# Edges loaded quad by quad ahead of the node features, and the first pass's keys, codes and feature casts put in another order

## The chip, the cores and the metric

The kernel runs on one core of one Trainium2 chip. A core has TensorE (matmuls; PE in the profile, PEld for its weight loads), VectorE (DVE), ScalarE (ACT), GpSimd (POOL) and SyncE (SP, which only issues DMAs here), each with its own instruction queue, which it works off in order. The metric is the device time of one execution in microseconds (us), the median of several runs.

## The reference

The inputs are 4096 node rows of 128 float32 numbers and 65,536 edges, each with a random source and a random destination node.

```python
output = np.zeros((num_nodes, dim), dtype=np.float32)
for i in range(len(edge_index_src)):
    output[edge_index_dst[i]] += node_features[edge_index_src[i]]
```

## The kernel before

The kernel sorts the edges by destination block and source block (32 blocks of 128 nodes each), with matmuls against one-hot matrices, and then multiplies the node features by 0/1 count matrices. Everything that the change touches lies in `_fast`, whose order on every engine is the order of the code (a manual schedule).

Loads. 128 partitions hold 512 edges each, as 64-bit numbers of which the low word counts. One DMA on SP's queue brings the destinations (`rawd`, L100), one on ScalarE's queue the sources (`raws`, L101). Right behind the destinations SP issues four DMAs of 512 KB for the node features X (`xf`, L109). VectorE fills the pads behind the edges (L102, L103).

Constants. `keep_busy(WARM)` runs 60 matmuls on a tile of ones whose result nobody reads (L127). GpSimd makes triangular matrices and iotas (L130 to L142), VectorE copies the iotas into a PSUM tile `psi` (L144 to L147), and GpSimd zeroes those parts of the two permutation tiles `p1` that no one-hot writes (L152 to L158): eight memsets.

Pass 1 sorts the edges in six "quads" q of up to 88 columns (22 groups of 4). For each quad: `dst_keys(q)` (VectorE) shifts the destinations to block numbers `kd`; `buckets1(q)` (VectorE, L210 with output `oh`) compares them with the iota, 128x2816 one-hot; `column_sums1(q)` (TensorE, 22 matmuls, L227) sums it, `scan(q)` (VectorE, L236) makes running sums; `counts(q)` is a generator that `count(q, n)` moves on by n steps: six steps of matmuls (L245, L249) with one ScalarE activation each (L252, `cum`), then 32 matmuls (L257, `psr`) and two ScalarE copies (L261) that give `rank1[q]`. `spread1(q)` (GpSimd, L273, four products) multiplies the one-hot by the words `kab` that `codes()` makes from both edge lists (VectorE L178 to L182, ScalarE L185). `move1(q)` makes the permutation one-hots in `p1` (VectorE, twelve L210 rows with output `p`) and permutes with TensorE (L296); ScalarE takes the result to `sbk` and `sa` (L300, L301). `move1` calls `during(q)`, which lays the next quads' counts and, with `beside`, pass 2's first group in between.

`x_part(i, 0)` casts a quarter of X on ScalarE (L195, 1 instruction); `x_part(i, 1)` makes its residual on GpSimd (L199, 2 instructions). They are needed when the products begin (L696), in the order of i.

The order ahead of the loop over `move1` is written out at L340 to L363. The code behind it is pass 2 (groups of destination blocks) and, from L767 on, 32 slots of one-hot (VectorE), block matmul (L689), ScalarE cast to `a` (L691) and product (L696).

Of the kernel before, what the change touches and what calls it, by code (L numbers as in the profile page):

```python
# [8 lines left out]
P = 128  # L9
F32 = mybir.dt.float32  # L10
F32R = mybir.dt.float32r
BF16 = mybir.dt.bfloat16
I32 = mybir.dt.int32
# [4 lines left out]
NB = 32  # L18
NCH = 24
NJ = 22  # L20
NH = NCH // 2
NQ = NCH // 4
# [1 line left out]
CODE0 = 0x2000  # L24
BIG = 4096.0
GROUPS = (4,) * 8
WARM = 60

LATER = (1, 3)
WHOLE = (1, 2)  # L30
# [6 lines left out]
WIN = ((0, 7, 0, 64), (7, 14, 4, 100), (14, NJ, 20, P))  # L37
# [45 lines left out]
def _fast(ctx, tc, X, src32, dst32, out, ident, fmax, flag_i, T):  # L83
# [13 lines left out]
    raws = raw[:, 2 * NT:4 * NT].rearrange("p (t w) -> p t w", w=2)  # L97
    code_i = raw[:, 4 * NT:].bitcast(U16)[:, :NT]
    sblk_i = raw[:, 4 * NT:].bitcast(U16)[:, NT:]
    nc.sync.dma_start(out=rawd[:, :T, :], in_=bass.AP(dst32, 0, [[2 * T, P], [2, T], [1, 2]]))  # L100
    nc.scalar.dma_start(out=raws[:, :T, :], in_=bass.AP(src32, 0, [[2 * T, P], [2, T], [1, 2]]))  # L101
    V.memset(rawd[:, T:, :], 4096)  # L102
    V.memset(raws[:, T:, :], 0)  # L103
    NX = 4
    BX = NB // NX
    xft = sb1.tile([P, NX, BX, P], F32, name="xf", tag="F")
    xf = [xft[:, i] for i in range(NX)]
    for i in range(NX):
        nc.sync.dma_start(out=xf[i], in_=X[i * BX * P:(i + 1) * BX * P, :].rearrange(  # L109
            "(s p) f -> p s f", p=P))  # L110


    identb = sb1.tile([P, P], BF16, name="identb")
# [4 lines left out]
    one = sb1.tile([P, 1], F32, name="one")  # L118
    iota = sb1.tile([P, P], U16, name="iota")
    iotas = sb1.tile([P, P], U16, name="iotas")  # L120
    V.tensor_copy(out=identb[:], in_=ident[:])
    G.memset(ones[:], 1.0)

    def keep_busy(n):
        psw = ps.tile([P, 512], F32, name="psw", tag="psA", bufs=4)
        for i in range(n):
            PE.matmul(out=psw[:, :P], lhsT=ones[:], rhs=ones[:], start=True, stop=True)  # L127

    keep_busy(WARM)
    G.affine_select(out=before[:], in_=ones[:], pattern=[[1, P]], base=0,  # L130
                    channel_multiplier=-1, compare_op=OP.is_gt, fill=0.0)
    G.affine_select(out=early[:], in_=before[:], pattern=[[1, P]], base=0,
# [9 lines left out]
    G.iota(iotax[:], pattern=[[2, NB // 2], [-1, 2]], base=1, channel_multiplier=0)  # L142
    psi = ps.tile([P, 4, P // 2], I32, name="psi", tag="psi", bufs=1)
    V.tensor_copy(out=psi[:, 0], in_=iota[:].bitcast(I32))  # L144
    V.tensor_copy(out=psi[:, 1], in_=iotas[:].bitcast(I32))
    V.tensor_copy(out=psi[:, 2], in_=iota4[:].rearrange("p s k -> p (s k)").bitcast(I32))
    V.tensor_copy(out=psi[:, 3, :NB // 2],  # L147
                  in_=iotax[:].rearrange("p s k -> p (s k)").bitcast(I32))
    piota, piotas = psi[:, 0].bitcast(U16), psi[:, 1].bitcast(U16)
    pswap = psi[:, 3].bitcast(U16)  # L150

    p1 = [sb1.tile([P, 2, NJ, P], BF16, name=f"p1{i}", tag=f"t2{i}") for i in range(2)]  # L152
    for t in p1:
        for j0, j1, m0, m1 in WIN:
            if m0 > 0:
                G.memset(t[:, :, j0:j1, :m0], 0.0)
            if m1 < P:
                G.memset(t[:, :, j0:j1, m1:], 0.0)  # L158

    p2a = sb1.tile([P, 2, NCH, P], BF16, name="p2a")  # L160

# [4 lines left out]
    kab = sb1.tile([P, NQ, NL], F32, name="kab", tag="K1")  # L166

    def by_quad(t):
        return t.rearrange("p (j q l) -> p q j l", q=NQ, l=4)

    def dst_keys(q):
        V.tensor_single_scalar(
            out=kd[:, q].rearrange("p (j l) k -> p j l k", l=4),
            in_=by_quad(d_lo)[:, q, :, :, None].to_broadcast([P, NJ, 4, 2]),
            scalar=7, op=OP.logical_shift_right)

    def codes():
        V.tensor_scalar(out=code_i, in0=s_lo, scalar1=127, scalar2=7,  # L178
                        op0=OP.bitwise_and, op1=OP.logical_shift_left)
        V.scalar_tensor_tensor(out=code_i, in0=d_lo, scalar=127, in1=code_i,  # L180
                               op0=OP.bitwise_and, op1=OP.bitwise_or)
        V.tensor_single_scalar(out=sblk_i, in_=s_lo, scalar=7, op=OP.logical_shift_right)  # L182
        words = kab[:].rearrange("p q n -> p (q n)")
        for dt, k, v, bias in ((U16, 1, code_i, CODE0), (BF16, 0, sblk_i, 1)):
            S.activation(  # L185
                out=words.bitcast(dt).rearrange("p (q j l k) -> p q j l k", q=NQ, l=4, k=2)[..., k],
                in_=by_quad(v), func=COPY, bias=float(bias))


    xr = [sb1.tile([P, NB // 2, 2, P], F32R, name=f"xr{h}") for h in range(2)]  # L190

    def x_part(i, v):
        blks = slice(i % 2 * BX, (i % 2 + 1) * BX)
        if v == 0:
            S.copy(out=xr[i // 2][:, blks, 0, :], in_=xf[i])  # L195
        else:
            for h in range(2):
                bs = slice(i % 2 * BX + h * BX // 2, i % 2 * BX + (h + 1) * BX // 2)
                G.tensor_tensor(out=xr[i // 2][:, bs, 1, :], op=OP.subtract,  # L199
                                in0=xf[i][:, h * BX // 2:(h + 1) * BX // 2],  # L200
                                in1=xr[i // 2][:, bs, 0, :])
# [16 lines left out]
    def buckets1(q):  # L218

        if q % 2 == 0:  # L220
            oh1[q // 2] = sb1.tile([P, 2, NL, NB], BF16, name="oh1", tag=f"o{q // 2}")
        onehot(oh1q(q), kd[:, q], NL, NB, io=pswap if q % 2 else piota)

    def column_sums1(q):
        pst = ps.tile([P, 512], F32, name="pst", tag=("ps2", "pso")[q % 2], bufs=1)
        for j in range(NJ):
            PE.matmul(out=pst[:, j:j + 1],  # L227
                      lhsT=oh1q(q)[:, 4 * j:4 * j + 4, :].rearrange("p l b -> p (l b)"),
                      rhs=ones[:, :1], start=True, stop=True)
        sums[q] = pst  # L230

    def scan(q):

        pst = sums[q]
        sums[q] = sb2.tile([P, NJ], BF16, name="sums")
        V.tensor_tensor_scan(out=sums[q][:], data0=ones[:, :NJ], data1=pst[:, :NJ], initial=0.0,  # L236
                             op0=OP.mult, op1=OP.add)
# [25 lines left out]
    def count(q, n=99):  # L263
        for _ in range(n):
            next(counting[q], None)
# [3 lines left out]
    def spread1(q):  # L269

        v1[q] = sb1.tile([P, NL, NB], F32, name="v1", tag=f"A{q % 2}")
        for l in range(4):
            G.tensor_tensor(out=v1[q][:, l::4], in0=oh1q(q)[:, l::4], op=OP.mult,  # L273
                            in1=kab[:, q, l::4, None].to_broadcast([P, NJ, NB]))
# [10 lines left out]
    def move1(q, meanwhile):  # L285
        tag, bufs = ("psA", 4) if q == NQ - 2 else ("misc", 1)
        psm = ps.tile([P, 512], F32, name="psm", tag=tag, bufs=bufs)
        for l in range(4):
            t = p1[l // 2]
            n = len([j for j in range(NJ) if j * NCH + q * 4 + l < T])  # L290
            for j0, j1, m0, m1 in WIN:
                j1 = min(j1, n)
                onehot(t[:, l % 2, j0:j1, m0:m1], rank1[q][:, l, j0:j1], j1 - j0, m1 - m0, m0=m0)
            meanwhile(l)
            for j in range(n):
                PE.matmul(out=psm[:, l * 64:(l + 1) * 64], lhsT=t[:, l % 2, j, :],  # L296
                          rhs=v1[q][:, 4 * j + l].bitcast(BF16),
                          start=j == 0, stop=j == n - 1)
        pv = psm[:, :256].rearrange("p (l b k) -> p l b k", l=4, k=2)
        S.copy(out=sbk[:, place(q), :], in_=pv[:, :, :, 0])  # L300
        S.copy(out=sa[:, place(q), :], in_=pv[:, :, :, 1])  # L301
# [37 lines left out]

    dst_keys(0)  # L340
    buckets1(0)
    column_sums1(0)
    x_part(0, 0)
    codes()
    scan(0)
    for q in range(1, NQ):
        dst_keys(q)
    spread1(0)
    count(0, 6)
    buckets1(1)  # L350
    column_sums1(1)
    spread1(1)
    buckets1(2)
# [1 line left out]
    scan(1)  # L355
    column_sums1(2)
    buckets1(3)
    x_part(0, 1)
    count(1, 6)
    x_part(1, 0)  # L360
    scan(2)
    column_sums1(3)
    x_part(1, 1)  # L363

    keys2 = {}
    p2b = [p2a[:, 0], p2a[:, 1]]
# [95 lines left out]
    def beside(q, l):  # L462

        if q == 2 and l == 2:
            start0()
            buckets0(0)
            buckets0(1)
        if q == 2 and l == 3:
            scan0(0)
            scan0(1)  # L470
        if q == 3 and l == 0:
            counts0(0)
            counts0(1)
        if q in (3, 4):
            if l == 1:
                buckets0(q - 1)
            if l == 2:
                scan0(q - 1)
            if l == 3:
                counts0(q - 1)  # L480
        if q == 5:
            if l == 1:
                ranks0(EARLY0[0], T0["x"][:, 384:], 2)
            if l == 2:
                buckets0(4)

    def during(q):

# [13 lines left out]
    for q in range(NQ):  # L502
        if q == NQ - 1:
            p2c = sb1.tile([P, 2, NCH, P], BF16, name="p2c", tag="o2")
            p2b += [p2c[:, 0], p2c[:, 1]]
        move1(q, during(q))
        if q + 4 < NQ:
            buckets1(q + 4)
            column_sums1(q + 4)
        if q < 2:  # L510
            x_part(q + 2, 0)
        if q + 2 < NQ:
            spread1(q + 2)

# [220 lines left out]
    for cs in EARLY0:  # L735
        permute0(0, cs)
    buckets0(NQ - 1)
    scan0(NQ - 1)
    counts0(NQ - 1)
    ranks0(place(4), T0["x"][:, 384:])  # L740
# [167 lines left out]
```

## Time and profile before

| | us |
|---|---|
| median of 3 runs | 277.62 (277.42 to 277.76) |
| the profiled execution | 277.6 |
| its span on the core | 275.9 |
| PE / DVE / ACT / POOL busy | 264.7 / 241.3 / 188.7 / 197.2 |
| all DMA | 3.15 MB read, 2.10 MB written |

The span runs from the first to the last recorded instruction; 1.7 us of the execution lie around it. Busy time of PE counts pipelined matmuls by modelled ends, so a busy PE is not a PE at its peak. A share over the whole span mixes the opening, pass 1, and the slots, which have different limits; the views below are therefore taken by stage. A row of the time line merges neighbouring instructions of one form: start, time, engine, line, operation, output and inputs, count, and in brackets the idle time before it and what ended that.

### The profile page before, as it was taken

Reading aid. Unit: us, or ns where it says so; the run is one execution under the profiler, and the core shown is the slowest. Engines: PE = TensorE matmul, PEld = TensorE weight load, DVE = VectorE, ACT = ScalarE, POOL = GpSimd, SP = SyncE. Lnnn points to the kernel's source line nnn. Section 1 sums busy time; section 2 is a strip of 40 time slices with the busy share of each in tenths; the row PEclk is TensorE's granted clock in tenths of the full one; section 3 lists DMA queues with packets and bytes.
Section 4 is the critical chain, followed back from the end, with each engine's and each line's share of the span. In section 5 each row is a group of like instructions: output and inputs, shape, how many; then the busy total and the mean of one; then the engine's idle time right before and its main releaser. Section 6 shows DMA issues by size and latency. Waiting matters only on the chain.

```text
span 275.9 us, 8028 instructions
## 1 busy us (share of the span) xinstructions
PE 264.7 (96%) x3466; PEld 223.3 (81%) x3466; DVE 241.3 (87%) x241; ACT 188.7 (68%) x403; POOL 197.2 (71%) x205
## 2 busy tenths in 40 slices
PE   7599999998999999999999999999999999999994
PEld 7488888986888888888888888888888788888872
DVE  3989986999999989999999999899898899889601
ACT  1867777247576857777668686857776776777761
POOL 7499999849599999999899998999699400000000
PEclk9999999999999999999999999999999999999998
DMA  7900000000000010001000100100010001001001
GB/s 229 230 2 4 5 4 4 2 5 0 2 2 1 2 40 0 2 1 40 2 0 2 38 2 1 40 4 0 2 38 2 0 2 38 2 0 40 0 5 39
DMA packets 8725, 5.77 MB, mean 21 GB/s; under 512 B 240, under 2 KB 8432, under 8 KB 8688
## 3 DMA queue, kind: packets, MB, share of 16 engines
q1 hardware_dynamic: 8272, 4.59, 5.9%
q10 hardware_dynamic: 416, 0.66, 0.8%
q8 instruction: 27, 0.44, 0.7%
q14 instruction: 10, 0.08, 0.1%
HBM read 3.15 MB, written 2.10 MB: 19 GB/s over the span
## 4 chain that ended last, share of the span: by engine, by line
PE 86%; ACT 5%; DVE 5%; DMA 2%; issue 1%; DVEq 0%; ACTq 0%
PE pso L696 44%; PE psa L689 20%; PE ps L616 4%; PE psm L296 3%; ACT cum L252 3%; PE psr L257 2%; PE psr L600 2%; DVE p L210 2%; DMA raw<-in_edge_index_dst_dram 2%; PE psb L565 2%; PE psc L249 2%; PE psc L245 2%; ACT cum L649 1%; PE psx L315 1%; DVE oh L210 1%
## 5 line engine op out<-in xcount | busy, mean ns | idle before, releaser
L691 ACT CAST a<-psa 128x512 fp32r<-128x512 f32 x256 | 131.7, 604 | 25.8 <-PE psa L689 25.7
L696 PE MATMUL pso<-a,xr 128*128 128x512 f32 x512 | 133.6, 403 | 0.2
L696 PEld LDWEIGHTS pso<-a,xr 128*128 128x128 f32 x512 | 91.0, 188 | 17.6 <-ACT a L691 1.6
L210 DVE TENSOR_TENSOR oh<-psi,slo 128x4096 bf16<-128x4096 uint16 (+1 forms) x34 | 73.4, 2159 | 8.2 <-PE psa L689 8.2
L210 DVE TENSOR_TENSOR oh<-psi,dlo 128x4096 bf16<-128x4096 uint16 (+1 forms) x34 | 73.3, 2155 | 0.0
L689 PE MATMUL psa<-oh 128*128 128x128 bf16 x1024 | 68.5, 219 | 0.6 <-ACT cum L649 0.6
L689 PEld LDWEIGHTS <-oh 128*128 128x128 bf16 x1024 | 58.0, 98 | 12.5 <-issue 12.2
L548 POOL TENSOR_TENSOR v<-oh,sa 128x512 bf16<-128x512 bf16 x42 | 42.7, 1054 | 1.8 <-DVE oh L539 1.8
L587 POOL TENSOR_TENSOR cum<-cum,oh 128x512 bf16<-128x512 bf16 x36 | 40.6, 1169 | 0.0
L273 POOL TENSOR_TENSOR v<-oh,kab 128x704 f32<-128x704 bf16 x24 | 32.9, 1403 | 5.5 <-ACT kab L185 4.4
L210 DVE TENSOR_TENSOR p<-psi,rank 128x448 bf16<-128x448 uint16 (+3 forms) x72 | 29.6, 479 | 0.0
L252 ACT ACTIVATE cum<-psc,minus 128x512 bf16<-128x512 f32 (+1 forms) x36 | 21.0, 650 | 2.4 <-PE psc L249 1.7
L578 POOL TENSOR_TENSOR cum<-cum,two 128x256 bf16<-128x256 bf16 x25 | 19.3, 770 | 4.5 <-ACT cum L567 2.9
L296 PE MATMUL psm<-v,p 128*128 128x64 bf16 x512 | 18.2, 193 | 0.2
L555 POOL TENSOR_TENSOR two<-oh 128x512 bf16<-128x512 bf16 x15 | 17.0, 1168 | 1.1 <-DVE oh L539 1.1
L296 PEld LDWEIGHTS <-p 128*128 128x128 bf16 x512 | 16.7, 98 | 0.4 <-issue 0.4
L582 POOL TENSOR_TENSOR cum<-cum,oh 128x512 bf16<-128x512 bf16 x15 | 17.0, 1164 | 0.0
L210 DVE TENSOR_TENSOR p2a<-psi,rank 128x3072 bf16<-128x3072 uint16 (+2 forms) x14 | 14.4, 1063 | 0.9 <-ACT rank L604 0.8
L210 DVE TENSOR_TENSOR p2c<-psi,rank 128x3072 bf16<-128x3072 uint16 x8 | 13.6, 1746 | 0.0
L249 PEld LDWEIGHTS <-sums 128*128 128x128 bf16 x126 | 10.0, 98 | 4.5 <-DVE sums L236 0.9
L249 PE MATMUL psc<-identb,sums 128*128 128x128 bf16 x126 | 12.6, 219 | 0.6 <-DVE sums L236 0.6
L245 PE MATMUL psc<-oh,early 128*128 128x512 bf16 (+1 forms) x36 | 13.0, 361 | 0.0
(105 smaller groups left out, 241.3 us busy)
## 6 DMA issues: line engine op xcount, KB each, us to landing
xf<-in_node_features_dram SPq DMA_DIRECT2D x4, 512.0 KB, 7.5
out_dram<-rows SPq DMA_DIRECT2D x7, 256.0 KB, 2.3
raw<-in_edge_index_src_dram ACTq DMA_DIRECT2D x1, 512.0 KB, 4.8
raw<-in_edge_index_dst_dram SPq DMA_DIRECT2D x1, 512.0 KB, 5.1
out_dram<-rows SPq DMA_DIRECT2D x1, 128.0 KB, 1.8
out_dram<-rows ACTq DMA_DIRECT2D x1, 128.0 KB, 2.1
```

What stands on the lines that cost most here:

```text
L210: V.tensor_tensor(out=dst.rearrange("p i (m k) -> p i m k", k=2), in0=io.rearrange("p i (m k) -> p i m k", k=2), in1=keys2[:, :, None, :]. ...
L245: PE.matmul(out=psc[:, :n * P], lhsT=early[:], rhs=oh1q(q)[:, 4 * j0:4 * (j0 + n), :].rearrange("p t b -> p (t b)"), start=True, stop=j0 + ...
L249: PE.matmul(out=psc[:, (j - j0) * P:(j - j0 + 1) * P], lhsT=sums[q][:, j - 1:j].to_broadcast([P, P]), rhs=identb[:], start=False, stop=j = ...
L252: S.activation(out=cum[:, :, 4 * j0:4 * (j0 + n)], func=RELU, bias=minus[:], in_=psc[:, :n * P].rearrange("p (t b) -> p b t", b=NB))
L273: G.tensor_tensor(out=v1[q][:, l::4], in0=oh1q(q)[:, l::4], op=OP.mult, in1=kab[:, q, l::4, None].to_broadcast([P, NJ, NB]))
L296: PE.matmul(out=psm[:, l * 64:(l + 1) * 64], lhsT=t[:, l % 2, j, :], rhs=v1[q][:, 4 * j + l].bitcast(BF16), start=j == 0, stop=j == n - 1)
L548: G.tensor_tensor(out=T2["v"][:, c:c + 4], in0=T2["o"][:, c:c + 4], op=OP.mult, in1=sa[:, c:c + 4, None, d0:d0 + 4].to_broadcast([P, 4, NB ...
L578: G.tensor_tensor(out=cum[:, :, 2 * i], in0=cum[:, :, 2 * i - 2], in1=two[:, :, i - 1], op=OP.add)
L587: G.tensor_tensor(out=flat("c")[:, c:c + 4], in0=flat("c")[:, c:c + 4], in1=flat("o")[:, c:c + 4], op=OP.mult)
L689: PE.matmul(out=psa[:, i * P:(i + 1) * P], lhsT=oh[:, 0, 4 * k + i, :], rhs=oh[:, 1, 4 * k + i, :], start=True, stop=True)
L691: S.copy(out=a[:, k, :], in_=psa[:])
L696: PE.matmul(out=pso[:], lhsT=xr[s // 16][:, s % 16, v, :], rhs=a[:, k, :], start=s == 0 and v == 0, stop=s == NB - 1 and v == 1)
```

## The change

The edge lists are cut by quad: a partition's first 88 edges are quad 0, the next 88 quad 1, then four quads of 84. Each list comes by three DMAs (quad 0; quad 1; quads 2 to 5) instead of one; only the latter four quads have pads. The DMAs of X move into `load_x()`, called behind `buckets1(0)`; ahead of them VectorE writes four elements of X's tile, which the DMAs therefore wait for. The zeroing of `p1` moves from GpSimd to VectorE and ahead of the cast of `identb`. WARM falls from 60 to 38; 6 matmuls of that kind come behind `column_sums1(0)` and 16 ahead of `column_sums1(1)`. ScalarE gets a small activation (`loaded`) near the start. Three of the four iota copies move behind `buckets1(0)`. `codes()` moves behind all `dst_keys`, and loses its ScalarE half, which becomes `words(a, b)`, called for quad 0 between the fourth and fifth step of `count(0)` and for the others behind the sixth. `buckets1(1)` moves up behind `codes()`. The casts of X's quarters move behind `move1(3)` (two) and `move1(4)` (two), the residuals of quarter 0 into `move1(5)` and those of quarter 1 behind `buckets0(5)`.

```diff
--- before.py
+++ after.py
@@ -24,7 +24,7 @@
...
 GROUPS = (4,) * 8
-WARM = 60
+WARM = 38
...
@@ -97,17 +97,30 @@
...
     sblk_i = raw[:, 4 * NT:].bitcast(U16)[:, NT:]
-    nc.sync.dma_start(out=rawd[:, :T, :], in_=bass.AP(dst32, 0, [[2 * T, P], [2, T], [1, 2]]))
-    nc.scalar.dma_start(out=raws[:, :T, :], in_=bass.AP(src32, 0, [[2 * T, P], [2, T], [1, 2]]))
-    V.memset(rawd[:, T:, :], 4096)
-    V.memset(raws[:, T:, :], 0)
+    QN = [(T // 4 + NQ - 1 - q) // NQ for q in range(NQ)]
+    runs = [(0, 1), (1, 2), (2, NQ)]
+    assert QN[0] <= NJ and sum(QN) * 4 == T
+    assert all(QN[q] == QN[a] for a, b in runs for q in range(a, b))
+    for a, b in runs:
+        at, n = 8 * sum(QN[:a]), 4 * QN[a]
+        for queue, of, to in ((nc.sync, dst32, rawd), (nc.scalar, src32, raws)):
+            queue.dma_start(
+                out=to.rearrange("p (q n) w -> p q n w", q=NQ)[:, a:b, :n],
+                in_=bass.AP(of, at, [[2 * T, P], [2 * n, b - a], [2, n], [1, 2]]))
+    for t, v in ((rawd, 4096), (raws, 0)):
+        for a, b in runs:
+            if QN[a] < NJ:
+                V.memset(t.rearrange("p (q n) w -> p q n w", q=NQ)[:, a:b, 4 * QN[a]:], v)
     NX = 4
...
     xf = [xft[:, i] for i in range(NX)]
-    for i in range(NX):
-        nc.sync.dma_start(out=xf[i], in_=X[i * BX * P:(i + 1) * BX * P, :].rearrange(
-            "(s p) f -> p s f", p=P))
+
+    def load_x():
+        V.memset(xft[:, :, 0, :1], 0.0)
+        for i in range(NX):
+            nc.sync.dma_start(out=xf[i], in_=X[i * BX * P:(i + 1) * BX * P, :].rearrange(
+                "(s p) f -> p s f", p=P))
...
@@ -118,8 +131,15 @@
...
     iotas = sb1.tile([P, P], U16, name="iotas")
+    G.memset(ones[:], 1.0)
+    p1 = [sb1.tile([P, 2, NJ, P], BF16, name=f"p1{i}", tag=f"t2{i}") for i in range(2)]
+    for t in p1:
+        for j0, j1, m0, m1 in WIN:
+            if m0 > 0:
+                V.memset(t[:, :, j0:j1, :m0], 0.0)
+            if m1 < P:
+                V.memset(t[:, :, j0:j1, m1:], 0.0)
     V.tensor_copy(out=identb[:], in_=ident[:])
-    G.memset(ones[:], 1.0)
...
@@ -127,6 +147,8 @@
...
     keep_busy(WARM)
+    loaded = sb1.tile([P, 1], F32, name="loaded")
+    S.activation(out=loaded[:], in_=ones[:, :1], func=RELU)
     G.affine_select(out=before[:], in_=ones[:], pattern=[[1, P]], base=0,
...
@@ -142,20 +164,13 @@
...
     V.tensor_copy(out=psi[:, 0], in_=iota[:].bitcast(I32))
-    V.tensor_copy(out=psi[:, 1], in_=iotas[:].bitcast(I32))
-    V.tensor_copy(out=psi[:, 2], in_=iota4[:].rearrange("p s k -> p (s k)").bitcast(I32))
-    V.tensor_copy(out=psi[:, 3, :NB // 2],
-                  in_=iotax[:].rearrange("p s k -> p (s k)").bitcast(I32))
+
+    def more_iotas(which):
+        for i, t in which:
+            V.tensor_copy(out=psi[:, i, :t.shape[1] // 2], in_=t.bitcast(I32))
+
     piota, piotas = psi[:, 0].bitcast(U16), psi[:, 1].bitcast(U16)
     pswap = psi[:, 3].bitcast(U16)
-
-    p1 = [sb1.tile([P, 2, NJ, P], BF16, name=f"p1{i}", tag=f"t2{i}") for i in range(2)]
-    for t in p1:
-        for j0, j1, m0, m1 in WIN:
-            if m0 > 0:
-                G.memset(t[:, :, j0:j1, :m0], 0.0)
-            if m1 < P:
-                G.memset(t[:, :, j0:j1, m1:], 0.0)
...
@@ -166,7 +181,7 @@
...
     def by_quad(t):
-        return t.rearrange("p (j q l) -> p q j l", q=NQ, l=4)
+        return t.rearrange("p (q j l) -> p q j l", q=NQ, l=4)
...
@@ -180,21 +195,23 @@
...
         V.tensor_single_scalar(out=sblk_i, in_=s_lo, scalar=7, op=OP.logical_shift_right)
-        words = kab[:].rearrange("p q n -> p (q n)")
+
+    def words(a, b):
+        ts = slice(a * NL, b * NL)
+        to = kab[:].rearrange("p q n -> p (q n)")
         for dt, k, v, bias in ((U16, 1, code_i, CODE0), (BF16, 0, sblk_i, 1)):
-            S.activation(
-                out=words.bitcast(dt).rearrange("p (q j l k) -> p q j l k", q=NQ, l=4, k=2)[..., k],
-                in_=by_quad(v), func=COPY, bias=float(bias))
+            S.activation(out=to.bitcast(dt).rearrange("p (n k) -> p n k", k=2)[:, ts, k],
+                         in_=v[:, ts], func=COPY, bias=float(bias))
...
-    def x_part(i, v):
+    def x_part(i, v, hs=(0, 1)):
         blks = slice(i % 2 * BX, (i % 2 + 1) * BX)
...
         else:
-            for h in range(2):
+            for h in hs:
                 bs = slice(i % 2 * BX + h * BX // 2, i % 2 * BX + (h + 1) * BX // 2)
...
@@ -287,7 +304,7 @@
...
             t = p1[l // 2]
-            n = len([j for j in range(NJ) if j * NCH + q * 4 + l < T])
+            n = QN[q]
             for j0, j1, m0, m1 in WIN:
...
@@ -339,15 +356,22 @@
...
     buckets1(0)
+    load_x()
     column_sums1(0)
-    x_part(0, 0)
-    codes()
+    keep_busy(6)
+    more_iotas([(1, iotas[:]), (2, iota4[:].rearrange("p s k -> p (s k)"))])
     scan(0)
+    more_iotas([(3, iotax[:].rearrange("p s k -> p (s k)"))])
     for q in range(1, NQ):
         dst_keys(q)
+    codes()
+    buckets1(1)
+    count(0, 4)
+    words(0, 1)
     spread1(0)
-    count(0, 6)
-    buckets1(1)
+    count(0, 2)
+    words(1, NQ)
+    keep_busy(16)
     column_sums1(1)
...
@@ -355,12 +379,9 @@
...
     buckets1(3)
-    x_part(0, 1)
     count(1, 6)
-    x_part(1, 0)
     scan(2)
     column_sums1(3)
-    x_part(1, 1)
...
@@ -479,10 +500,14 @@
...
         if q == 5:
+            if l == 0:
+                x_part(0, 1, (0,))
             if l == 1:
...
                 buckets0(4)
+            if l == 3:
+                x_part(0, 1, (1,))
...
@@ -507,8 +532,9 @@
...
             column_sums1(q + 4)
-        if q < 2:
-            x_part(q + 2, 0)
+        if q in (3, 4):
+            x_part(2 * q - 6, 0)
+            x_part(2 * q - 5, 0)
         if q + 2 < NQ:
...
@@ -735,6 +761,7 @@
...
     buckets0(NQ - 1)
+    x_part(1, 1)
     scan0(NQ - 1)
...
     ranks0(place(4), T0["x"][:, 384:])
```

## Rows read from the trace of the kernel before

**Rows 1.** Chain of waits in order of time, to 22 us: start, us, what.
```profile
0.92 5.08 DMA raw<-in_edge_index_dst_dram
10.52 3.34 ACT cum L252 x6
13.90 1.41 PE psr L257 x32
16.34 3.37 ACT cum L252 x6
19.75 1.42 PE psr L257 x32
```

**Rows 2.** Busy time by stage: stretch, length, busy us per engine (instructions), clock, DMA.
```profile
20.00:45.00 25.00, 24.76 (x589) 22.06 (x587) 22.74 (x56) 19.02 (x41) 24.48 (x20) 1.00 0.01 4
66.00:276.00 210.00, 205.28 (x2129) 170.62 (x2126) 186.17 (x113) 148.59 (x315) 141.78 (x143) 1.00 0.04 12
```

**Rows 3.** Time line of the opening: VectorE, then TensorE and ScalarE.
```profile
1.03 0.09 DVE L103 MEMSET raw<- 128x32 int32 x1
1.62 0.29 DVE L121 CAST identb<-ident 128x128 bf16<-128x128 f32 x1 [0.50 <-POOL ident masks.py:199]
6.02 0.42 DVE L172 TENSOR_SCALAR kd<-raw 128x176 uint16<-128x176 uint16 x1 [2.35 <-DMA raw<-in_edge_index_dst_dram]
6.47 1.62 DVE L210 TENSOR_TENSOR oh<-psi,kd 128x2816 bf16<-128x2816 uint16 x1
8.01 0.42 DVE L178 TENSOR_SCALAR raw<-raw 128x528 uint16<-128x528 uint16 x1
9.44 0.19 DVE L236 TENSOR_TENSOR_SCAN sums<-ones,pst 128x22 bf16<-128x22 bf16 x1
9.55 0.87 DVE L172 TENSOR_SCALAR kd<-raw 128x176 uint16<-128x176 uint16 x5
...
8.15 0.70 PE L227 MATMUL pst<-ones,oh 128*128 128x1 bf16 x22 [1.76 <-DVE oh L210]
...
9.21 1.44 ACT L185 ACTIVATE kab<-raw 128x528 uint16<-128x528 uint16 x2 [0.37 <-DVE raw L180]
```

**Rows 4.** Time line of GpSimd in the opening.
```profile
3.20 0.84 POOL L158 MEMSET p<- 128x896 bf16 x1
5.97 0.36 POOL L156 MEMSET p<- 128x320 bf16 x1
```

**Rows 5.** Stretches by DMA, all engines; the last number is GB/s.
```profile
1.80:3.00 1.20, 1.20 (x14) 1.20 (x12) 0.51 (x3) 0.83 (x1) 1.13 (x7) 1.00 0.77 119
3.00:5.25 2.25, 2.25 (x29) 2.25 (x28) 0.46 (x3) 0.00 (x0) 2.25 (x7) 1.00 0.98 398
7.00:12.00 5.00, 3.25 (x49) 2.37 (x49) 4.97 (x12) 3.83 (x6) 1.26 (x1) 1.00 1.16 290
```

**Rows 6.** DMA issues of the page: kind, count, KB each, us from issue to landing.
```profile
xf<-in_node_features_dram SPq DMA_DIRECT2D x4, 512.0 KB, 7.5
...
out_dram<-rows SPq DMA_DIRECT2D x1, 128.0 KB, 1.8
```

**Rows 7.** Warm-up matmuls of L127 alone, TensorE, two stretches.
```profile
2.00:4.00 2.00, 2.00 (x22) 1.00 0.81 260
5.00:6.00 1.00, 1.00 (x21) 1.00 1.02 333
```

**Rows 8.** Time line of casts, residuals and what stands near them: ScalarE, VectorE, GpSimd.
```profile
19.56 1.07 ACT L195 CAST xr<-xf 128x1024 fp32r<-128x1024 f32 x1
...
21.64 4.97 POOL L199 TENSOR_TENSOR xr<-xf,xr 128x512 fp32r<-128x512 f32 x4
...
53.41 0.50 ACT L424 CAST rank<-ps 128x32 bf16<-128x32 f32 x4 [1.12 <-PE ps L420]
...
55.39 1.27 DVE L210 TENSOR_TENSOR p2a<-psi,rank 128x1024 bf16<-128x1024 uint16 x2
...
71.48 8.18 POOL L572 TENSOR_TENSOR cum<-cum,oh 128x256 bf16<-128x256 bf16 x11 [2.93 <-issue]
```

## The prediction

> **What bounds the kernel now.** I read the stages first. From 20 to 45 us TensorE is busy 24.76 of 25 us, with VectorE at 22.74 and GpSimd at 24.48 [rows 2]; from 66 us to the end it is TensorE again, 205.28 of 210. There the chain of waits runs through TensorE, so work taken off another engine brings nothing by itself; but all of it starts when the opening lets it. The opening is what the change rearranges, so I read the chain of its first 22 us [rows 1]. It is one string: the destinations' DMA from 0.92 to 6.00, keys and one-hot of quad 0 on VectorE, its sums, six `cum` on ScalarE (10.52 to 13.86), 32 rank matmuls from 13.90, six `cum` of quad 1 (16.34 to 19.71), rank matmuls of quad 1 at 19.75. From there TensorE has work without a gap. I therefore forecast by how much the row at 19.75 moves, and let the rest follow it one for one.
>
> On VectorE the reader sees the wait: it is idle 2.35 us until the destinations land at 6.02, then `kd` and `oh`, and then the three instructions of `codes` from 8.01, which hold the first scan to 9.44 although the column sums that it needs ended at 8.15 + 0.70 = 8.85 [rows 3].
>
> **When quad 0 lands.** In before, 119 GB/s come from 1.80 to 3.00 us (143 KB) and 398 GB/s afterwards [rows 5]. Both edge lists are 1049 KB; 143 KB + 2.25 us x 398 GB/s puts their last byte near 5.28, and `kd` starts at 6.02: 0.74 us from the last byte to the waiting engine. Quad 0 is 128 x 704 bytes of each list, 180 KB together. On the same ramp these are there at 3.00 + 37 KB / 398 GB/s = 3.1, and seen at 3.84. The trace has no load of this size. The nearest small one, a store of 128 KB, takes 1.8 us [rows 6], which would give 0.92 + 1.8 = 2.72; that is the lower bound. For an upper one I take 0.5 us more than 3.84, as the packets shrink from 4 KB to 704 bytes and packets of X's 512 bytes go at 290 GB/s, not 398 [rows 5]. I take 3.84, because the ramp is that of the same queues at the same moment.
>
> **What VectorE does before that.** It gets the eight memsets of `p1`, 2 x 1664 = 3328 bf16 elements. On GpSimd they last from 3.20 to 6.33 [rows 4], and no wait hung on them. No row shows a large memset on VectorE. Its 16-bit one-hots run 2816 elements in 1.62 us, 1.74 per ns [rows 3]: by that rate 1.9 us. At GpSimd's rate they take 3.13; at one element per VectorE memset step as its 32-element rows show (the two rows lie 0.04 us apart, the second is in [rows 3]), 4.2. I take 1.9, the rate of this engine at this width, as the zeros are 16-bit data. From the end of the pads' memsets (about 1.07) VectorE is then ready for `kd` at 1.07 + 1.9 + 0.29 (cast of `identb` [rows 3]) + 0.29 (first iota copy, taken like it) = 3.55, ahead of the 3.84: hidden. The cover is 0.29 us; each us beyond it costs a us.
>
> A rule of the Trainium skill speaks against this part: "VectorE: DVE Perf Modes", section "Zero memsets can be issued as uint32 (trn2)", says that a memset takes one cycle per element whatever the width, unless the zeros are issued as 4-byte words. No row here decides it. By that page an estimate is 3328 / 0.96 GHz = 3.5 us when unpacked, and VectorE would be ready at 5.15; packed, 1.7 us, and it stays hidden.
>
> **From landing to the first scan.** `kd` of quad 0 took 0.42 us while GpSimd's last memset ran (5.97 to 6.33 [rows 4]); the five later ones take 0.87 together [rows 3]. GpSimd is idle now, so I take 0.27 to the next start. Then 1.62 for `oh`, 0.06 to TensorE, 0.70 of column sums, 0.04 to the scan: 3.84 + 0.27 + 1.62 + 0.06 + 0.70 + 0.04 = 6.53, against 9.44. `codes` no longer stands in front of the scan, and two iota copies (at most 0.29 each) fit beside the 0.70 of sums. The gain at the scan is 2.91.
>
> (The skill's "SBUF — State Buffer", section "Who interferes with whom", has such narrow single-source VectorE operations share a port with GpSimd, which fits the 0.42. Without that effect the sum would lose 0.15.)
>
> **From the scan to quad 1's ranks.** VectorE now has, behind the scan: one iota copy (0.12, a quarter as wide as the others; an estimate), five `kd` (0.87), `codes` (9.44 - 8.01 = 1.43), then `buckets1(1)` (1.62) [rows 3]. That ends 4.04 behind the scan's start, where before `buckets1(1)` came first and needed 0.11 + 0.87 + 1.62 = 2.6. `column_sums1(1)` waits for it and stands on TensorE's queue ahead of quad 0's rank matmuls, so these start at 4.04 + 0.04 + 0.55 = 4.63 behind the scan (the sums' 0.70 less an estimated 0.15 of overlap); before 13.90 - 9.44 = 4.46. The other road to them, ScalarE, is no longer than before: `cum` starts 0.4 earlier, as `kab` (1.44 for two full-width writes [rows 3]) is no longer in front; `words(0, 1)`, a sixth of that width, costs between 0.24 (scaled) and 1.44, and I take 0.4, giving 4.4. The rest of the words, at most 1.44, lies beside the 1.41 of the rank matmuls. So `psr` of quad 0 starts at 6.53 + 4.63 = 11.16. From `psr` to the second `cum` group it is 16.34 - 13.90 = 2.44 and from there 19.75 - 16.34 = 3.41 [rows 1]; `buckets1(2)` is ready 5.6 behind the scan and the column sums that need it start at 5.9. The row at 19.75 moves to 11.16 + 2.44 + 3.41 = 17.01: 2.74 earlier.
>
> The added matmuls: 6 of warm-up type behind the first sums take 0.3 us of the 0.3 or so until the scan has been read, and delay `cum` by 0.1, which lies in ScalarE's slack of 0.25; 16 more end before `column_sums1(1)` can start. WARM 38 ends near 5.0: the rate of L127 is 22 matmuls touched in 2 us early, 21 in 1 us later [rows 7], half speed and full speed, the granted clock reading 1.00 in both. Those are the levels of 1.2 and 2.4 GHz. TensorE is idle some 0.8 us until its sums; in before it was idle 1.76 [rows 3] and the sums ran no slower than later.
>
> **The moved feature work.** X's DMAs start about 2 us later than quad 0's landing and need 2.10 MB / 290 GB/s = 7.2 us; nobody needs X before the casts near 45. SP's queue has nothing else until the first output. Four casts (1.07 us each [rows 8], two per place) land on ScalarE behind `sa` of quads 3 and 4. Behind quad 4 they push the four `rank` copies of pass 2 from 53.41 to about 54.4; these end at 54.9, and VectorE takes their result at 55.39 [rows 8]. Hidden by 0.5 us. Residuals: GpSimd gets four of 4.97 / 4 = 1.24 us near 53 to 61, and it has an idle 2.93 before 71.48 [rows 8] that swallows what is left of them. Between 20 and 45 GpSimd loses 4.97 us of residuals, but TensorE is the bound there, so nothing is gained.
>
> **Sum.** 277.6 - 2.74 = 274.9, against the profiled execution; that stands 0.02 from the median, so the forecast for the median is the same.
>
> **Rivals.**
> *The memsets hold VectorE.* At 3.13 to 4.2 us, `kd` starts at 4.8 to 5.85 instead of 3.84; the gain falls to 1.8 to 0.7, time 275.8 to 276.9, with 276.3 in the middle. For it: the memset rows of both engines; against it: the rate of other 16-bit work. It decides from 2.2 us of memsets on.
> *The late quads' edges come late* (the one that ends slower). `dst_keys(2)` needs the third DMA 0.4 behind the scan, at 6.9; all of `codes`, `words(0, 1)`, two of quad 0's `cum` and `buckets1(1)` queue behind it on VectorE and ScalarE. The edges alone, with X away, should be in by 1.8 + 1049 KB / 290 GB/s + 0.74 = 6.2. But 512 KB loads of X took 7.5 us in the median from issue to landing, behind others [rows 6]; such a landing from 1.7 on would be 9.2, cost 2.3 and leave 277.2. From 9.6 on the change loses; at 10.6 it is 278.6.
> *TensorE falls back to the lower clock* in the new gaps. The count matmuls of quad 0 (about 0.44 per `cum` of 0.57) would double and become the bound: 6 x 0.3 for it and 0.5 for the sums, gain 0.4 to 0.6, time 277.1. Against it: the 1.76 us gap in before.
> *The shift is not carried*: the casts or residuals end last near 47 to 62 us and eat it. The casts would have to be 0.5 us later than worked out just to show, 3 us to eat all: 277.4.
>
> **Numbers.** Forecast 0.62; memsets 0.18; late edges 0.09 (0.05 of it slower); lower clock 0.04; not carried 0.07. Low end: landing at 2.72 makes the ready time of 3.55 decide, gain 3.0, and 0.3 more if the second sums do not hold the ranks: 274.2. High end: 276.9, which takes in the memsets at their dearest. A measurement of this kernel can tell about 0.2%, 0.55 us, from no change. Faster 0.87, same 0.07, slower 0.06.
>
> **What would show it.** The first `kd` near 3.8 with VectorE idle just before it says that landing decides; VectorE's memset rows just before it, with no idle time, say the first rival. The first scan should start near 6.5 with `codes` behind it; `psr` of quad 0 near 11.2, released by the column sums and not by `cum`; `psr` of quad 1 near 17.0. An idle VectorE before the third `kd` means late edges; L227 or L249 rows at double length mean the clock. The stretch from 17.0 to the end should be as long as 19.75 to the end was. I am wrong if the first `kd` moves by 2 us and the end doesn't.

## The result and the profile after

The changed kernel takes 274.94 us (median of 5, 274.46 to 275.17) beside 277.61 us for the kernel before (277.38 to 277.76): ratio 0.9902, 95% interval 0.9888 to 0.9917, or 2.67 us less. The forecast was 274.9. The profiled execution took 275.11 us with a span of 273.5, against 277.6 and 275.9.

The chain of waits of the changed kernel, in order of time, answers to [rows 1] (`issue` is time in which the engine waited for nothing that the profile shows):

```profile
...
1.85 5.18 DMA raw<-in_edge_index_dst_dram
7.05 0.27 DVE kd L187 x2
...
8.16 0.71 DVE raw L195
8.87 0.34 DVE raw L197
9.21 1.54 DVE oh L227
10.76 0.05 issue
10.80 0.70 PE pst L244 x22
11.50 1.27 PE psr L274 x32
...
13.80 3.38 ACT cum L269 x6
17.18 0.04 issue
17.22 1.41 PE psr L274 x32
```

The rank matmuls of quad 1, which the forecast took as its mark, moved from 19.75 to 17.22, 2.53 us. What follows is as long as it was: 275.9 - 19.75 = 256.2 before, 273.5 - 17.22 = 256.3 after. But the chain is not the one forecast. It doesn't begin with quad 0. It begins with the third DMA of the destinations, quads 2 to 5, issued at 1.85 and seen at 7.03. The rank matmuls of quad 0 then wait for the column sums of quad 1 (10.80), as forecast.

VectorE's time line, against [rows 3]:

```profile
1.17 0.43 DVE L141 MEMSET p<- 128x448 uint32 x1
1.55 0.08 DVE L139 MEMSET p<- 128x28 uint32 x1
...
2.83 0.35 DVE L142 CAST identb<-ident 128x128 bf16<-128x128 f32 x1
2.91 0.39 DVE L166 COPY psi<-iota 128x64 int32<-128x64 int32 x1
3.34 0.25 DVE L187 TENSOR_SCALAR kd<-raw 128x176 uint16<-128x176 uint16 x1
...
6.15 0.20 DVE L253 TENSOR_TENSOR_SCAN sums<-ones,pst 128x22 bf16<-128x22 bf16 x1 [0.23 <-PE pst L244]
...
7.05 0.73 DVE L187 TENSOR_SCALAR kd<-raw 128x176 uint16<-128x176 uint16 x4 [0.47 <-DMA raw<-in_edge_index_dst_dram]
```

VectorE has no idle time ahead of the first `kd` at 3.34; the iota copy ended at 3.30. The zeros go out as 4-byte words, half the elements, and the eight of them last from 1.17 to 2.91. The first scan starts at 6.15, the third `kd` waits 0.47 us for the edges.

### The profile page after: what moved, and what is told of

Same layout as the page of the kernel before. It is cut to its first block, busy times and chain, and to the rows that moved or that the text cites. A ratio compares the mean times of both kernels' runs of the same rounds, so it can differ in the third digit from the quotient of the medians.

```text
span 273.5 us, 8041 instructions
## 1 busy us (share of the span) xinstructions
PE 265.2 (97%) x3466; PEld 223.8 (82%) x3466; DVE 242.5 (89%) x250; ACT 188.8 (69%) x406; POOL 194.1 (71%) x197
## 3 DMA queue, kind: packets, MB, share of 16 engines
HBM read 3.15 MB, written 2.10 MB: 19 GB/s over the span
## 4 chain that ended last, share of the span: by engine, by line
PE 87%; DVE 5%; ACT 4%; DMA 2%; issue 1%; SPq 0%; DVEq 0%; ACTq 0%
PE pso L722 45%; PE psa L715 21%; PE ps L642 4%; PE psm L313 3%; PE psr L274 2%; PE psr L626 2%; DVE p L227 2%; DMA raw<-in_edge_index_dst_dram 2%; PE psb L591 2%; PE psc L262 2%; PE psc L266 2%; ACT cum L269 1%; ACT cum L675 1%; PE psx L332 1%; PE pst L244 1%
```

## The experiments

As the opening sets everything behind it, each experiment gives the start of quad 1's rank matmuls in its profile, called the mark, beside the time. The ratios are to the kernel before, measured beside it on the same chip; the twelve runs come from three chips, so two variants are best compared by their ratios. In some of these kernels single executions differ by 1 to 4 us; where the profile of such a kernel isn't of one of its fastest executions, it shows TensorE at half rate for longer in the opening, because its clock falls there or rises late. The spread stands in brackets behind the median. Starts of rank matmuls are those of the time line; a chain counts them from the end of the work ahead of them, which is 0.13 later for quad 0 in the one above.

### What carries the gain

**Whole edge lists** (the split undone, with the old interleaving of the quads):

```diff
-    for a, b in runs:
...
-            queue.dma_start(
-                out=to.rearrange("p (q n) w -> p q n w", q=NQ)[:, a:b, :n],
...
+    nc.sync.dma_start(out=rawd[:, :T, :], in_=bass.AP(dst32, 0, [[2 * T, P], [2, T], [1, 2]]))
+    nc.scalar.dma_start(out=raws[:, :T, :], in_=bass.AP(src32, 0, [[2 * T, P], [2, T], [1, 2]]))
```

> The changed kernel with each edge list in one DMA again (and its quads interleaved as before), everything else as changed, X still held back. Theory A (quad 0's early landing carries the gain): the first kd waits for the whole list, to about 5.95; first scan near 8.8, psr of quad 0 near 13.4, psr of quad 1 near 19.2, time about 277.0. Rival B (the new order on VectorE and ScalarE carries it): time stays at 275.0 to 275.5.

277.76 us (276.67 to 278.88), ratio 1.0006 (0.9988 to 1.0024): the whole gain is gone, 0.8 more than theory A had; the mark is at 19.97. The first `kd` waited to 5.91 and the scan came at 8.66, both as theory A said. But quad 0's rank matmuls started at 14.12, not 13.4. TensorE by stretch in this run (length, busy time and instructions, granted clock, busy share of the DMA engines, GB/s):

```profile
0.00:6.00 6.00, 3.68 (x38) 1.00 0.54 175
6.00:8.00 2.00, 0.13 (x4) 0.92 0.00 0
8.00:10.00 2.00, 1.78 (x32) 0.50 0.34 102
10.00:12.00 2.00, 2.00 (x18) 0.73 1.15 319
```

The 38 warm-up matmuls ended at 5.00 and the column sums came at 7.87. After these 2.87 us of nothing the granted clock was 0.50, the lower of its two levels (1.2 GHz), and groups of count matmuls that take 0.22 elsewhere in these chains took 0.43. So this run undid two things. The next one separates them.

**Whole edge lists with 60 warm-up matmuls** (the edit above, and this one):

```diff
-WARM = 38
+WARM = 60
```

> The changed kernel with whole edge lists, as in the run above that undid the split, and WARM at 60 again, so that TensorE has work until about 6.4. Theory A (there the clock fell, because TensorE had nothing to do from 5.0 to 7.87): granted clock 1.00 from 8 to 12, first scan near 8.7, psr of quad 0 near 13.3 instead of 14.12, psr of quad 1 near 19.2, time about 277.0. Rival B (the count matmuls were slow for another reason): they stay at 0.4 per cum step in place of 0.2, time 277.7.

276.50 us (276.45 to 276.78), ratio 0.9955 (0.9940 to 0.9969). The granted clock is 1.00 throughout the opening. TensorE in this run:

```profile
7.92 0.70 PE L235 MATMUL pst<-ones,oh 128*128 128x1 bf16 x22 [0.29 <-DVE xf L111]
...
13.30 1.41 PE L265 MATMUL psr<-cum,identb 128*128 128x88 bf16 x32
...
19.15 1.41 PE L265 MATMUL psr<-cum,identb 128*128 128x88 bf16 x32 [0.34 <-ACT cum L260]
```

The sums follow the one-hot at once, the scan starts at 8.65, quad 0's ranks at 13.30, quad 1's at 19.15. Theory A holds, with the time 0.5 below what it gave. This is the change without the split: 0.60 of the 2.53 us at the mark. The split brings the rest, 19.15 - 17.19 = 1.96 on the same chip (next run); with 60 warm-up matmuls in both it is 19.15 - 17.27 = 1.88 (the run with 60 in the changed kernel, below). By the time the shares are less sure. The medians on this chip (277.86 before, 276.50 here, 275.08 changed) give 1.36 us without the split and 1.42 for it; the lowest executions (277.19, 276.45, 274.48) give 0.74 and 1.97, as the kernel before varied up to 279.08 there. So the split is the larger part by the profiles, and about half by the medians.

**The changed kernel again**, on that chip:

> The changed kernel unaltered, beside the other runs of this call, so that they are compared on one chip. 274.6 to 275.2; psr of quad 1 within 0.3 of 17.2, the spread coming from the landing of quad 0 (3.3 to 3.6) and of the last edges (7.0 to 7.3).

275.08 us (274.48 to 276.53), ratio 0.9912 (0.9889 to 0.9934); mark at 17.19. VectorE, TensorE and ScalarE:

```profile
6.33 0.88 DVE L187 TENSOR_SCALAR kd<-raw 128x176 uint16<-128x176 uint16 x5
...
7.00 0.49 PE L266 MATMUL psc<-identb,sums 128*128 128x128 bf16 x3 [0.22 <-issue]
...
7.59 2.42 ACT L269 ACTIVATE cum<-psc,minus 128x512 bf16<-128x512 f32 x4 [3.76 <-PE psc L266]
...
17.19 1.41 PE L274 MATMUL psr<-cum,identb 128*128 128x88 bf16 x32 [0.34 <-ACT cum L269]
```

Here the last edges were in time, which the expectation didn't have, and another road was as long. TensorE ran at half rate until past 7: the three `psc` matmuls at 7.00 took 0.49 us, where the first profile of this kernel has 0.33 for them at 6.81. So the first `cum` started at 7.59 instead of 7.24. The mark is the same within 0.03. Two roads of nearly equal length end there: the last edges with VectorE, and the warm-up with `cum`.

**codes ahead of the scan:**

```diff
+    codes()
     scan(0)
...
-    codes()
```

> The changed kernel with the three VectorE instructions of codes ahead of the first scan, where they stood before. Theory A (codes, which needs the last edges at about 7.05, would hold the scan): scan near 8.7 instead of 6.15, psr of quad 0 near 13.2, psr of quad 1 near 19.0, time 276.7, up to 278 if the clock falls in the gap. Rival B (the order of VectorE doesn't matter, since the sum of its work up to buckets1(1) is the same): psr of quad 0 stays near 11.5, time within 0.3 of the changed kernel.

277.41 us (276.24 to 279.31), ratio 0.9982 (0.9962 to 1.0003). VectorE waited 1.67 us for the sources and started `codes` at 7.46, the scan at 8.90:

```profile
7.46 0.43 DVE L193 TENSOR_SCALAR raw<-raw 128x528 uint16<-128x528 uint16 x1 [1.67 <-DMA raw<-in_edge_index_src_dram]
...
8.90 0.19 DVE L253 TENSOR_TENSOR_SCAN sums<-ones,pst 128x22 bf16<-128x22 bf16 x1
```

The mark came at 20.26, as the granted clock read 0.50 from 10 to 12. Theory A holds, within its upper figure; even the lowest execution, 276.24, is 1.2 above the changed kernel. With `codes` in its old place the split is worth 0.45 us of the 2.8 by the medians, and by the interval of the ratio anything from nothing to about 1. Part of the loss is the clock; what it would be at full clock isn't shown.

**Zeros back on GpSimd** (the loop stands behind the iotas again):

```diff
-                V.memset(t[:, :, j0:j1, :m0], 0.0)
+                G.memset(t[:, :, j0:j1, :m0], 0.0)
```

> The changed kernel with the eight zero memsets of p1 back on GpSimd, behind its iotas. VectorE is then ready for the first kd at about 2.8 instead of 3.30. Theory A (the landing of quad 0 near 3.3 and of the last edges at 7.03 decide): first kd still near 3.3, perhaps 0.2 longer beside GpSimd's memsets, the third kd still near 7.05, time within 0.15 of the changed kernel. Rival B (the memsets on VectorE hold the first kd): first kd near 2.9 and time 0.4 lower.

276.33 us by all six executions (275.57 to 279.89); 275.76 without the highest, which the ratio, 0.9928 (0.9905 to 0.9951), leaves out. The profiled execution took 278.32, with the mark at 20.46. Theory A has the start of the first `kd` right and the rest wrong; rival B is wrong as well. The time line of VectorE, then of GpSimd, in this run:

```profile
3.29 3.15 DVE L188 TENSOR_SCALAR kd<-raw 128x176 uint16<-128x176 uint16 x1 [0.57 <-DMA raw<-in_edge_index_dst_dram]
6.47 1.62 DVE L228 TENSOR_TENSOR oh<-psi,kd 128x2816 bf16<-128x2816 uint16 x1
...
3.20 0.84 POOL L174 MEMSET p<- 128x896 bf16 x1
...
5.97 0.36 POOL L172 MEMSET p<- 128x320 bf16 x1
```

The edges are there at 3.29, the first `kd` starts, and takes 3.15 us instead of 0.25: it ends at 6.44, just behind GpSimd's last memset (6.33). The 0.42 of the first `kd` in [rows 3] was the tail of the same thing. With the zeros on GpSimd the early landing is worthless in such an execution, and TensorE, 2.80 us without work, lost its clock as well (0.54 from 10 to 12). The executions fall in two groups, 275.6 to 275.8 and 276.9 to 279.9, so half of them kept most of the gain; `kd` starts 0.09 behind the first memset here, so landing a little earlier may escape it, but no profile of the faster group was taken.

**Zeros of one tile on GpSimd**, to see what ends the block:

```diff
-    for t in p1:
+    for t in p1[:1]:
...
+    for t in p1[1:]:
...
+                G.memset(t[:, :, j0:j1, :m0], 0.0)
```

> The changed kernel with the zero memsets of one of the two p1 tiles back on GpSimd, behind its iotas, where they run from 3.20 to about 4.75. Theory A (the first kd, once it starts beside GpSimd's row of memsets, gets on only when that row ends): kd starts near 3.3 and ends near 4.8, half of the 3.15 us that it took beside all eight; psr of quad 0 near 12.3, time about 275.9. Rival B (the 3.15 us had to do with the landing of the edges, such as DMA writes into the tile that kd reads): kd still lasts about 3 us.

275.16 us (275.05 to 276.36), ratio 0.9903 (0.9886 to 0.9920), the changed kernel's time. VectorE and GpSimd:

```profile
3.46 0.74 DVE L194 TENSOR_SCALAR kd<-raw 128x176 uint16<-128x176 uint16 x1 [0.69 <-DMA raw<-in_edge_index_dst_dram]
...
3.26 0.84 POOL L180 MEMSET p<- 128x896 bf16 x1
4.04 0.25 POOL L178 MEMSET p<- 128x56 bf16 x1
4.12 0.50 POOL L180 MEMSET p<- 128x392 bf16 x1
```

The same two short memsets in the kernel before, where VectorE had nothing to do beside them:

```profile
3.98 0.14 POOL L156 MEMSET p<- 128x56 bf16 x1
4.06 0.42 POOL L158 MEMSET p<- 128x392 bf16 x1
```

`kd` ended at 4.20, not at the end of GpSimd's row (4.93): it came through at the first change of instruction there, and the two memsets around it are longer (0.25 and 0.50 for 0.14 and 0.42). So theory A's rule is wrong, and rival B too: in these two profiles a memset on GpSimd held the VectorE instruction, and at a boundary either won. In the run with all eight, VectorE lost at each of the seven boundaries. What decides it isn't shown. (The profiled execution, 276.36, is the slowest of its kernel: its matmuls ran at half rate until 10.6, which moved the mark to 18.53.) This fits the Trainium skill's "SBUF — State Buffer", section "Who interferes with whom": VectorE's copies, casts and `tensor_scalar` operations can take a port pair that it shares with GpSimd; whoever issues first has it for the whole instruction, and the other is blocked. The trace agrees with 0.74 for one instruction; the 3.15 are eight in a row.

### What holds the new opening

**Long runs** (five quads of 88 edges and one of 72 in a partition, so that quads 1 to 4 are one contiguous run):

```diff
-    QN = [(T // 4 + NQ - 1 - q) // NQ for q in range(NQ)]
-    runs = [(0, 1), (1, 2), (2, NQ)]
+    QN = [NJ] * (NQ - 1) + [T // 4 - NJ * (NQ - 1)]
+    runs = [(0, 1), (1, NQ - 1), (NQ - 1, NQ)]
```

> The changed kernel with quads of 88, 88, 88, 88, 88 and 72 edges per partition, so that quads 1 to 4 come as one contiguous run of 2816 bytes per partition instead of one of 704 and four of 672. Theory A (many short packets make the last edges late): no wait before the third kd, psr of quad 0 bound by cum at about 10.95 instead of 11.37, time 0.4 lower, 274.5. Rival B (the third DMA of a queue is late by its place, not its packets): the third kd still waits until about 7 and the time stays 274.9.

274.06 us (273.95 to 274.71), ratio 0.9863 (0.9844 to 0.9883), below the changed kernel's interval. VectorE:

```profile
3.56 0.25 DVE L187 TENSOR_SCALAR kd<-raw 128x176 uint16<-128x176 uint16 x1 [0.25 <-DMA raw<-in_edge_index_dst_dram]
...
6.44 0.89 DVE L187 TENSOR_SCALAR kd<-raw 128x176 uint16<-128x176 uint16 x5
```

No wait within the five `kd`, although quad 0 was seen 0.22 later than in the changed kernel's profile; the mark came at 16.76, 0.46 earlier. By the time theory A holds. The profile owes its mark to two things, though: the warm-up matmuls sped up early in this execution (3.55 us for the 38, not 4.23), so that the first `cum` started at 7.07. With a first `cum` at 7.59, as in the changed kernel's second profile, `cum` would have held quad 0's ranks to 11.34, as it did there, and they start at 10.91 here. The DMA rates of the changed kernel by stretch, to be laid beside the 398 GB/s of [rows 5]:

```profile
1.80:3.00 1.20, 1.20 (x15) 1.20 (x13) 1.16 (x8) 0.66 (x1) 1.13 (x7) 1.00 0.76 197
3.00:5.25 2.25, 2.25 (x24) 2.25 (x22) 2.17 (x5) 0.83 (x2) 0.26 (x2) 1.00 0.91 206
```

The start is quicker than before (197 against 119), and then the short packets go at 206. That is one execution: the second profile has 280 GB/s from 3.00 to 5.25 with the same packets, the kernel with long runs 307. The landing separates them better. From issue to landing the third DMA of the destinations took 4.4 to 5.4 us in the nine profiles with short runs, and the last two DMAs of the destinations 4.3 to 4.5 in the two with long runs.

**X not held:**

```diff
-        V.memset(xft[:, :, 0, :1], 0.0)
...
+    load_x()
...
-    load_x()
```

The call now stands right behind the edges' DMAs.

> The changed kernel with X's four DMAs issued right behind the edges' and not held for VectorE. Theory A (X queues behind the destinations on its own queue and takes little of the last sources' time): third kd still near 7.05, codes at most 0.2 later, time within 0.2. Rival B (X shares the 16 engines with the last edges): the last sources land 1 us or more later, codes waits for them, time 0.7 to 1.2 higher.

276.41 us (275.17 to 278.83 over 12 executions), ratio 0.9965 (0.9938 to 0.9992). In the profiled execution (275.44) theory A holds: the third `kd` waited 0.60 us, to 7.28, and the mark came at 17.45, 0.23 later. But the median is 1.5 above the changed kernel's, and the execution that the profile shows is one of the fastest. So leaving X unheld is not free, against theory A. The five executions from 277.15 up have a mean granted clock of 0.983 to 0.994, the other seven 0.997 to 1.000, so the clock had a part in those five. Whether the edges were still later in some, as rival B says, isn't shown.

**Without the six matmuls:**

```diff
     column_sums1(0)
-    keep_busy(6)
```

> The changed kernel without the 6 warm-up matmuls behind the first column sums. Theory A (they stand in front of the count matmuls and end at 6.8 where the scan has been read at 6.4): first cum at about 6.9 instead of 7.24 to 7.59; psr of quad 0 between 10.85 and 11.4, depending on the last edges; time 0.0 to 0.4 lower. Rival B (TensorE needs them for its clock): granted clock under 1.00 between 6 and 12 and time 1 or more higher.

274.78 us (274.74 to 275.23), ratio 0.9892 (0.9875 to 0.9909). The first `cum` started at 6.85 instead of 7.24, the granted clock stayed 1.00, and the mark at 17.23 did not move, because the third `kd` waited 0.47 again. Theory A, at the lower end of its 0.0 to 0.4 by the mark and within it by the time: the six stand in the way of a road that isn't the longest.

**60 warm-up matmuls in the changed kernel:**

> The changed kernel with 60 warm-up matmuls at the start instead of 38. Theory A (with quad 0 early they stand in front of the first column sums): the first column sums begin at 6.0 to 6.8 instead of 5.34, the first cum 0.7 to 1.3 later, psr of quad 0 at 11.9 to 12.4, time 0.6 to 1.1 higher. Rival B (the faster clock that they bring makes up for it): time within 0.2 of the changed kernel.

275.62 us (275.10 to 276.46), ratio 0.9927 (0.9908 to 0.9947). Quad 0 was seen at 3.61 here; the first column sums began at 6.05, 0.53 behind their one-hot's end, and the first `cum` at 7.58, 0.34 later than in the changed kernel's profile; quad 0's ranks at 11.43 and the mark at 17.27 moved by 0.06 and 0.05 only, since the third `kd` no longer had to wait. By the profile rival B's figure, by the median 0.7 more, theory A's; one profile doesn't decide it.

**X's casts and residuals in pass 1:**

```diff
     count(1, 6)
+    x_part(0, 0)
+    x_part(0, 1)
...
-        if q in (3, 4):
-            x_part(2 * q - 6, 0)
-            x_part(2 * q - 5, 0)
+        if q < 3:
+            x_part(q + 1, 0)
...
```

> The changed kernel with X's casts and the residuals of the first two quarters back in pass 1: cast and residual of quarter 0 behind the first six cum of quad 1, the other casts behind move1(0), (1), (2), the residual of quarter 1 behind the product of quad 2. Theory A (TensorE is the bound there and around the last quads alike, so their place costs nothing): time within 0.2 of the changed kernel. Rival B (they hold quads in pass 1, or their new place brings something): 0.5 or more higher.

274.79 us (274.41 to 275.05), ratio 0.9889 (0.9872 to 0.9907), 0.3 below the changed kernel on the same chip and within its spread; the mark at 17.16. Theory A in the main (it had 0.2): this part of the change moves nothing in the time.

**Together** (long runs, no six, all six `cum` ahead of the words, quad 0's ranks ahead of the second column sums, the scan of quad 2 inside `move1(0)`):

```diff
-    count(0, 4)
+    count(0, 6)
     words(0, 1)
...
+    count(0)
     words(1, NQ)
...
     column_sums1(1)
...
```

> A version meant to be faster: quads of five times 88 and once 72 (long runs), no 6 matmuls, all six cum of quad 0 ahead of the words of quad 0, quad 0's rank matmuls ahead of column_sums1(1), the scan of quad 2 inside move1(0). Theory A (the opening up to quad 1's ranks sets the time one for one): psr of quad 0 near 10.3, psr of quad 1 near 16.2, time 273.4 to 273.7. Rival B (VectorE's three buckets and the first permutation one-hots are the next bound): psr of quad 1 stays near 16.7 and the time near 274.1.

274.12 us (274.09 to 274.34), ratio 0.9867 (0.9850 to 0.9884): no better than the long runs alone; rival B. Quad 0's ranks start at 10.49, the mark stands at 16.89. The chain of this run, from the scan of quad 2 on:

```profile
15.74 0.04 DVE sums L253
15.78 0.08 issue
15.86 0.67 DVE p L227 x2
...
17.26 1.54 DVE p L227 x5
```

With quad 0's ranks earlier, VectorE is late next: its one-hots for three quads and then those of the first permutation.

## Why the forecast was right, point by point

The time was right (274.94 for 274.9), the mark nearly (17.22 for 17.01), and the stretch behind it within 0.1. Two terms of the sum were off, the scan 0.38 early and the way from it to quad 0's ranks 0.59 long, and they nearly cancelled: that the time fits to 0.04 is luck, while most of the gain is not. The stretch behind the mark kept its length although the chain in it runs through VectorE from 45 to 54 us, and not, as forecast, through TensorE without a gap.

**When quad 0 lands** was mis-sized: forecast 3.84, seen at 3.29 to 3.62 in the six profiles where VectorE waited for it, and at 3.22 and 3.23 or before in two others. The ramp of before was too slow a guess: with quad 0 ahead, 197 GB/s came from 1.80 to 3.00, not 119. VectorE was ready at 3.30 for a forecast 3.55, with 1.74 us of zeros for a forecast 1.9. So the cover of 0.29 that the forecast gave the zeros shrank to about nothing in the changed kernel's profile, and either could end last. The scan came at 6.15 for 6.53, 0.38 too good.

**The memsets' rate.** The rival with slow zeros fell, since they go as 4-byte words: 448 in 0.43 us. The forecast's 1.9 was near the 1.74 for another reason, a rate of 16-bit one-hots. The Trainium skill's "VectorE: DVE Perf Modes", section "Zero memsets can be issued as uint32 (trn2)", had both outcomes; by its one element per cycle an estimate for 1664 words is 1.7 us, and the trace agrees.

**What the zeros cost where they were** was the step that failed without showing in the total. The forecast wrote the shared port off at 0.15 us, from the 0.42 of one `kd`. Left on GpSimd, they met the early `kd` in the one profile taken and held it to 6.44, 3.15 us instead of 0.25. The move to VectorE was counted as neutral and hidden; without it half of the executions kept most of the gain (275.6 to 275.8) and half lost 1.8 us or more of it. Moving one tile's zeros was enough for the time.

**The last edges** failed in size: 6.2 forecast, 7.03 measured, with 206 GB/s from 3.00 to 5.25 and not X's 290. The rival of the late edges was thus there in part, with 0.47 of VectorE's time. It is why the earlier scan gave nothing: in the changed kernel's profile its lead of 0.38 is spent in the wait at 7.05. In the second profile the edges were in time, as forecast, and the late `cum` took the lead instead.

**From the scan to quad 1's ranks**: the road through `codes`, `buckets1(1)` and its column sums was named rightly as the longer one, and its pieces agree: from quad 0's ranks, 11.37 in the time line, 2.43 to the second `cum` and 3.42 to the mark, for 2.44 and 3.41 forecast. The term in front of it was mis-sized: from the scan to quad 0's ranks 5.22 instead of 4.63, 0.47 of it the wait. The six matmuls were priced at 0.1; they cost the first `cum` 0.39, more than the 0.25 of slack that the forecast had, and the mark still didn't move, as the run without them shows.

**The clock** was given 0.04, on the ground that 1.76 us without work did no harm. In the changed kernel's profiles there is no such gap, since the 38 matmuls end at 5.55 and not at 5.0. But in three of the variants the profiled execution lost it: after 2.87 us without work (whole lists), after 2.80 (zeros on GpSimd), and after 2.51 (`codes` first). The 38 matmuls are enough because quad 0 is early: with whole lists 38 lost the clock and 60 kept it.

**The moved feature work** was right. The casts at 45.01 and 49.65 pushed the `rank` copies of pass 2 to 51.55, 0.67 later than [rows 8] less 2.53. They end at 52.06, and VectorE takes them at 52.95. ScalarE's time line in the changed kernel:

```profile
49.65 2.00 ACT L212 CAST xr<-xf 128x1024 fp32r<-128x1024 f32 x2
51.55 0.51 ACT L445 CAST rank<-ps 128x32 bf16<-128x32 f32 x4
```

and its chain, where the one-hot made from them stands:

```profile
52.95 1.19 DVE p2a L227 x2
```

## What to carry to other kernels

When one part of an opening is made earlier, look at what runs beside its new place, not its old one: here the zeros had been harmless on GpSimd because VectorE was waiting beside them, and the shorter warm-up is long enough only while quad 0 comes early. Cut a load so that the first piece is small and the rest stays in long runs; cutting the rest into short runs too gave back part of what the first piece won, about 0.4% of the time here. And when two roads of nearly equal length meet, a profile names one of them: taking work off the other, as with the six matmuls, brings nothing.

## What the runs showed of the hardware

A VectorE instruction that takes 0.25 us alone took 3.15 us beside eight GpSimd memsets of 0.14 to 0.84 us in a row, and in another run, beside four, it came through at the first boundary (0.74).

The point at which the warm-up matmuls speed up differs between executions: the same 38 took 3.55 us in the kernel with long runs and 4.23 in the changed kernel. The granted clock read 1.00 while they ran at half rate, as in the first of [rows 7], so that column alone doesn't tell the level; the length of the rows does. TensorE's time line in the kernel with long runs:

```profile
1.32 3.55 PE L147 MATMUL psw<-ones 128*128 128x128 bf16 x38 [1.32 <-POOL ones L134]
```

and in the changed kernel:

```profile
1.32 4.23 PE L147 MATMUL psw<-ones 128*128 128x128 bf16 x38 [1.32 <-POOL ones L134]
```
